# Edge tile, two attention heads side by side, and one layer's memory keys and values as three-pass products

## The chip, the core and the metric

The kernel runs on one core of a Trainium2 chip. Times are device microseconds of that core. The median of the runs of the kernel before the change is 2687.13 us (three runs, 2686.7 to 2687.75).

## What is computed

A network of three layers on one sequence of 512 tokens with 1024 features, in float32: an RWKV-7 layer, a Conformer convolution layer (both with attention to 256 memory tokens and a gated convolutional feed-forward), and a hybrid layer with gated linear attention and a "forget attention" of 8 heads. The parts that the change touches:

```python
memn = rmsnorm(mem, mem_norm_g)                      # mem: 256 x 1024
# memory_cross_attention, in layers 0 and 1:
kv = memn @ w_kv                                     # 1024 x 2048
km = kv[..., :D].reshape(B, -1, XATTN_HEADS, XATTN_HEAD_DIM)
vm = kv[..., D:].reshape(B, -1, XATTN_HEADS, XATTN_HEAD_DIM)
...
# fox_attention, in the hybrid layer: 8 heads of 64 features, blocks of 128 queries
for i in range(S // Q_BLOCK):
    lo, hi = i * Q_BLOCK, (i + 1) * Q_BLOCK
    logits = jnp.einsum('bhqd,bhkd->bhqk', qh[:, :, lo:hi], kh[:, :, :hi]) * scale
    logits = logits + c[:, :, lo:hi, None] - c[:, :, None, :hi]
    mask = jnp.arange(hi)[None, :] <= jnp.arange(lo, hi)[:, None]
    p = jax.nn.softmax(jnp.where(mask, logits, -jnp.inf), axis=-1)
    outs.append(jnp.einsum('bhqk,bhkd->bhqd', p, vh[:, :, :hi]))
```

## The kernel before

Activations lie with features on partitions (8 tiles of 128 x 512, k or m = 0 to 7). A float32 product is made of three matmuls on split operands (`acc3`, L212): each operand is a high part (type float32r) and the rest; high x high (L218), streamed rest x high (L219) and high x rest (L220) add up in one PSUM bank. The names in the trace are in the order output, streamed operand, stationary operand; `ah`, `al`, `bh`, `bl` are the two sides of the pool `act`, `h` the tiles of `home`, `mid` those of the ffn pool, `yh` and `yl` those of `hyo`, `mh` and `ml` the mixed inputs of the first layer.

`Weights` (L34) streams 398 weights tiles of up to 128 x 1024 in a fixed order. SyncE loads each into one of two raw buffers; `_split` (L54) makes the high part on ScalarE (L63) and the rest on VectorE, or on GpSimd for a list of numbers `W_POOL` (L64), into three pairs of buffers; the raw buffer is free after the split. Two kinds of weights, `WHOLE` (L31: memory keys and values of layer 1), aren't split: their raw tile is the operand of one whole float32 matmul (L216), which the profile records as two instructions, and the raw buffer is free when the last of these has read it.

`linear` (L222) runs 8 (or 22) k-steps of `acc3` for each output tile m; a projection of 8 k-steps over 512 columns has 24 matmuls. The framework orders each engine's queue by a simulated timeline within the program's priorities, so TensorE may run matmuls of a later step while an earlier one isn't ready.

Layer 1, `conformer` (L574): `lin` projects the input (conv_w_in), `memory` (L422) loads and scales the memory tokens and sums their squares, here with 32 recorded matmuls of one column (L436); then, for j = 0 to 7, two projections, one step of `memory_keys` (L459: one output tile, 8 products of 256 columns) and a depthwise convolution (L613). Behind them `memory_values` (L481: 32 products of 512 columns, in 8 steps) fills TensorE's time while VectorE and ScalarE do the layer norm over the convolution's result (L662 to L692); conv_w_out follows and needs that result split, chunk by chunk (`al`, L246). Layer 0 has the same keys and values as split products inside `rwkv`, between the steps of its recurrence.

Hybrid layer, `fox_pair` (L945): a generator for two heads (p = 0 to 3). Its steps: projection of q and k (16 k-steps of `acc3`), norms (L962 to L971), then for each head of the pair in turn the scores of all four query blocks (L984) with their softmax (L986 to L993), and the transposes (L1000), copies (L1003) and value products (L1004). A head has 64 of the 128 partitions of q and k, and writes 64 of the 128 partitions of the output. `FOX` (L1631) gives, for each pair, the order of the steps: `c` is the next step of this pair, `Q` and `n` the projection and the norms of the next pair, `G` one projection of the gates (20 in all, 14 of them here).

Addresses, as the framework's allocator gives them to this program: the left-hand pools begin above a reserved scratch for dynamic DMA of 16,384 bytes per partition; weights buffers, `home` (from byte 73,024) and the ffn pool (105,792 to 134,464) begin on multiples of 64. The right-hand pools hang from the top: `act` (147,424 to 229,344; tiles of 2048 bytes) and the first layer's `mix` begin 32 past a multiple of 64. `fb` (L716) takes 32 bytes, so that the pools behind it in the hybrid layer (`hyf`, and `hyo`, 108,128 to 140,896) begin 32 past a multiple of 64 too.

## Time and profile before

| | us |
|---|---|
| median of three runs | 2687.13 |
| the profiled execution, whole | 2691.29 |
| its span, first to last instruction | 2688.5 |
| TensorE busy in it | 2581.6 |
| VectorE, ScalarE, GpSimd busy | 1463.5, 1067.4, 368.3 |

[...] Outside the span lie 2.8 us of the profiled execution. A matmul's duration in the profile overlaps with that of its successor, so the pace of a run of matmuls is read from the starts.

### The profile page before, as it was taken

What the parts mean: (1) busy time and instruction counts of PE and PEld (TensorE: products, weight loads), DVE (VectorE), ACT (ScalarE), POOL (GpSimd) and SP (SyncE); (2) the same over time, 40 slices, a digit from 0 to 9 for tenths busy, and PEclk for the clock granted to TensorE, in tenths of its full rate; (3) what the DMA queues carried; (4) which work ended last, traced back from release to release, by engine and by line L of the source; (5) the groups of instructions that cost most, each with busy time, mean ns of one, the idle gap of its engine ahead of it and who ended that gap; (6) DMA issues with size and microseconds to landing.
All of it is one profiled execution on the core that took longest, in us unless ns stands there. A gap on an engine that the chain in (4) does not pass through costs nothing.

```text
span 2688.5 us, 33718 instructions
## 1 busy us (share of the span) xinstructions
PE 2581.6 (96%) x13436; PEld 2000.3 (74%) x13436; DVE 1463.5 (54%) x2140; ACT 1067.4 (40%) x1709; POOL 368.3 (14%) x362
## 2 busy tenths in 40 slices
PE   6987889899999999999999999999999999999998
PEld 5666767677888888765677888887786677888886
DVE  7584887745677733322654777534324456655522
ACT  6754355534444423312443444323223344433321
POOL 3037422430100001000202000001010000100000
PEclk9997569899999999999999999999998899999999
DMA  3211001321332233443311322232211113322232
GB/s 109 71 51 63 2 17 41 124 94 40 102 99 95 92 92 102 128 124 93 111 63 63 110 94 94 88 91 75 71 63 56 40 40 101 96 94 94 92 93 81
DMA packets 69596, 218.33 MB, mean 81 GB/s; under 512 B 9228, under 2 KB 14749, under 8 KB 69439
## 3 DMA queue, kind: packets, MB, share of 16 engines
q1 hardware_dynamic: 69438, 216.19, 25.6%
q8 instruction: 105, 1.72, 0.3%
q14 instruction: 53, 0.43, 0.1%
HBM read 205.69 MB, written 2.10 MB: 77 GB/s over the span
## 4 chain that ended last, share of the span: by engine, by line
PE 88%; DVE 7%; ACT 2%; POOL 2%; issue 1%; DMA 0%; DVEq 0%; POOLq 0%; ACTq 0%
PE mm L218 24%; PE mm L220 24%; PE mm L219 24%; PE aux L613 2%; PE mm L216 2%; PE aux L321 1%; PE mm L1004 1%; PE mm L1371 1%; POOL inv L1320 1%; POOL inv L1319 1%; PE aux L984 1%; DVE u L1159 1%; DVE h L1289 0%; DVE ml L246 0%; PE aux L1000 0%
## 5 line engine op out<-in xcount | busy, mean ns | idle before, releaser
L63 ACT ACTIVATE wh<-wr 128x1024 fp32r<-128x1024 f32 (+5 forms) x382 | 388.2, 1019 | 788.3 <-PE mm L219 629.0
L64 DVE TENSOR_TENSOR wl<-wr,wh 128x1024 fp32r<-128x1024 f32 (+3 forms) x341 | 401.7, 1179 | 294.8 <-ACT wh L63 292.5
L218 PE MATMUL mm<-ah,wh 128*128 128x512 f32 x1088 | 432.8, 398 | 0.9 <-ACT wh L63 0.9
L219 PE MATMUL mm<-al,wh 128*128 128x512 f32 x1088 | 431.2, 397 | 2.4 <-DVE al L246 2.4
L220 PE MATMUL mm<-ah,wl 128*128 128x512 f32 x1088 | 430.0, 397 | 0.6 <-DVE wl L64 0.5
L218 PE MATMUL mm<-bh,wh 128*128 128x512 f32 (+1 forms) x1000 | 399.7, 401 | 0.0
L219 PE MATMUL mm<-bl,wh 128*128 128x512 f32 (+1 forms) x1000 | 398.1, 398 | 0.0
L220 PE MATMUL mm<-bh,wl 128*128 128x512 f32 (+1 forms) x1000 | 396.6, 398 | 0.0
L218 PEld LDWEIGHTS mm<-ah,wh 128*128 128x128 f32 x1088 | 204.7, 188 | 54.2 <-ACT wh L63 3.7
L219 PEld LDWEIGHTS mm<-al,wh 128*128 128x128 f32 x1088 | 204.8, 188 | 52.8 <-DVE al L246 3.0
L220 PEld LDWEIGHTS mm<-ah,wl 128*128 128x128 f32 x1088 | 204.9, 188 | 50.9 <-DVE wl L64 2.3
L218 PEld LDWEIGHTS mm<-bh,wh 128*128 128x128 f32 (+1 forms) x1000 | 188.6, 189 | 49.9 <-issue 3.9
L269 POOL TENSOR_TENSOR acc<-acc,sq 128x512 f32<-128x512 f32 x55 | 88.3, 1605 | 1001.0 <-ACT sq L268 1000.6
L219 PEld LDWEIGHTS mm<-bl,wh 128*128 128x128 f32 (+1 forms) x1000 | 188.4, 188 | 48.1 <-issue 3.3
L220 PEld LDWEIGHTS mm<-bh,wl 128*128 128x128 f32 (+1 forms) x1000 | 188.1, 188 | 47.9 <-issue 1.7
L381 DVE TENSOR_TENSOR u<-mm,rs 128x512 f32<-128x512 f32 x132 | 90.9, 691 | 176.9 <-PE mm L220 176.7
L64 POOL TENSOR_TENSOR wl<-wr,wh 128x1024 fp32r<-128x1024 f32 (+2 forms) x41 | 98.9, 2413 | 589.6 <-ACT wh L63 589.3
L366 DVE TENSOR_TENSOR x<-x,mm 128x512 f32<-128x512 f32 x56 | 38.5, 687 | 138.8 <-PE mm L220 138.7
L219 PE MATMUL mm<-ml,wh 128*128 128x512 f32 (+1 forms) x224 | 91.4, 409 | 2.4 <-DVE ml L246 2.4
L218 PE MATMUL mm<-mh,wh 128*128 128x512 f32 (+1 forms) x224 | 87.7, 413 | 5.2 <-ACT mh L245 3.7
L220 PE MATMUL mm<-mh,wl 128*128 128x512 f32 (+1 forms) x224 | 90.1, 405 | 1.3 <-DVE wl L64 1.3
L395 ACT ACTIVATE uy<-uy 128x512 f32<-128x512 f32 x66 | 41.6, 632 | 122.5 <-DVE uy L393 122.4
(494 smaller groups left out, 4051.3 us busy)
## 6 DMA issues: line engine op xcount, KB each, us to landing
wr<-ffn_w_in SPq DMA_DIRECT2D x132, 512.0 KB, 3.4
wr<-ffn_w_out SPq DMA_DIRECT2D x48, 448.0 KB, 3.3
wr<-ffn_w_out SPq DMA_DIRECT2D x24, 512.0 KB, 3.5
wr<-hy_g SPq DMA_DIRECT2D x20, 512.0 KB, 3.5
wr<-kv_k SPq DMA_DIRECT2D x16, 512.0 KB, 3.5
wr<-kv_v SPq DMA_DIRECT2D x16, 512.0 KB, 3.5
wr<-xattn_w_q SPq DMA_DIRECT2D x16, 512.0 KB, 3.4
wr<-xattn_w_o SPq DMA_DIRECT2D x16, 512.0 KB, 3.4
```

Source lines behind the costliest of these rows:

```text
L63: self.last_hi = self.nc.scalar.activation(out=hi[:r, :c], in_=t[:r, :c], func=AF.Copy).ins
L64: (self.nc.gpsimd if i in W_POOL else self.nc.vector).tensor_tensor(out=lo[:r, :c], in0=t[:r, :c], in1=f32(hi[:r, :c]), op=ALU.subtract)
L216: self.last_mm = mm(out, lhsT=w[0], rhs=x[0], start=first, stop=last).ins
L218: mm(out, lhsT=w[0], rhs=x[0], start=first, stop=False)
L219: mm(out, lhsT=w[0], rhs=x[1], start=False, stop=False)
L220: mm(out, lhsT=w[1], rhs=x[0], start=False, stop=last)
L269: nc.gpsimd.tensor_tensor(out=self.sq, in0=self.sq, in1=s, op=ALU.add)
L321: self.last_bcast = self.nc.tensor.matmul(ps[:, b * P : (b + 1) * P], lhsT=col[:, b : b + 1].to_broadcast([P, P]), rhs=self.ident, start=T ...
L366: self.nc.vector.tensor_tensor(out=self.x[m], in0=self.x[m], in1=ps, op=ALU.add)
L381: nc.vector.tensor_tensor(out=u, in0=ps, in1=rs, op=ALU.mult)
L395: self.last_silu = nc.scalar.activation(out=y, in_=y, func=AF.Silu if l < 2 else AF.Gelu_apprx_tanh).ins
L613: nc.tensor.matmul(ps[32 * g : 32 * g + 32, 4 * e :], lhsT=w[:, 8 * g + e], rhs=t[:, g, : T - 4 * e], start=(e == 0), stop=(e == 7), skip_ ...
```

## The change

Four things. A spare tile `edge` of 168 float32 per partition is laid at the top of the right-hand side, `fb` takes 16 instead of 8 columns, and the reserved scratch for dynamic DMA is 1,024 instead of 16,384 bytes. `WHOLE` goes: the 16 weights tiles `kv_k1`, `kv_v1` are split like all others, and layer 1's `memory` makes split tiles (twice the bytes) and sums the squares on VectorE, with one pair of column sums on TensorE (`token_sums`). `fox_pair` works on both heads of a pair at once, one query block after the other: scores of block qb for both heads, then transposes, copies and value products of block qb - 1 for both. `FOX` is rewritten for the new steps (norms, four blocks, the last values), with the same 14 gate projections. The order of the weights stays the same. The diff:

```diff
@@ -25,10 +25,6 @@
 
 def f32(ap):
     return ap.bitcast(F32)
-
-
-
-WHOLE = "kv_k1", "kv_v1"
 
 
 class Weights:
@@ -54,10 +50,6 @@
     def _split(self, i):
         key, ap = self.order[i]
         t, r, c = self.raws[i]
-        if key[0] in WHOLE:
-            self.raws[i] = None
-            self.parts.append((t[:r, :c].rearrange("p (a b) -> p a b", b=ap.shape[2]),))
-            return
         hi = self.pool.tile([P, 1024], F32R, tag="whi", bufs=self.bufs, name=f"wh{i}")
         lo = self.pool.tile([P, 1024], F32R, tag="wlo", bufs=self.bufs, name=f"wl{i}")
         self.last_hi = self.nc.scalar.activation(out=hi[:r, :c], in_=t[:r, :c], func=AF.Copy).ins
@@ -98,6 +90,8 @@
         self.ctx, self.tc, self.nc, self.a, self.vec_at = ctx, tc, tc.nc, args, vec_at
         nc = self.nc
         self.keep = ctx.enter_context(tc.tile_pool(name="keep", bufs=1))
+
+        ctx.enter_context(tc.tile_pool(name="edge", bufs=1, side="right")).tile([P, 168], F32, name="edge")
         self.wpool = ctx.enter_context(tc.tile_pool(name="wts", bufs=1))
         self.tmp = ctx.enter_context(tc.tile_pool(name="tmp", bufs=1))
         self.hpool = ctx.enter_context(tc.tile_pool(name="home", bufs=1, reuse_waits="tile"))
@@ -212,9 +206,6 @@
     def acc3(self, out, w, x, first, last):
 
         mm = self.nc.tensor.matmul
-        if len(w) == 1:
-            self.last_mm = mm(out, lhsT=w[0], rhs=x[0], start=first, stop=last).ins
-            return
         mm(out, lhsT=w[0], rhs=x[0], start=first, stop=False)
         mm(out, lhsT=w[0], rhs=x[1], start=False, stop=False)
         mm(out, lhsT=w[1], rhs=x[0], start=False, stop=last)
@@ -419,25 +410,17 @@
 
             self.linear(f"ffn_w_out{l}", KF, list(range(KD)), lambda k: mid[k], out, group=1)
 
-    def memory(self, pool, split):
+    def memory(self, pool):
 
         nc = self.nc
         self.memn = []
         acc = pool.tile([P, MEM], F32, name="macc")
-        ps = None if split else self.aux()
         for k in range(KD):
             raw = self.t512("u", 3, n=MEM)
             nc.sync.dma_start(out=raw, in_=self.a["mem"][:, k, :])
             g = self.vec("g_mem", k)
-            s = self.t512("sq", 2, n=MEM) if k or not split else acc
+            s = self.t512("sq", 2, n=MEM) if k else acc
             nc.scalar.activation(out=s, in_=raw, func=AF.Square)
-            if not split:
-                for b in range(2):
-                    nc.tensor.matmul(ps[:, 2 * k + b : 2 * k + b + 1], lhsT=s[:, b * P : (b + 1) * P], rhs=self.ones[:, 0:1], start=True, stop=True)
-                t = pool.tile([P, MEM], F32, name=f"mn{k}")
-                nc.scalar.activation(out=t, in_=raw, func=AF.Copy, scale=g)
-                self.memn.append((t,))
-                continue
             if k:
                 nc.vector.tensor_tensor(out=acc, in0=acc, in1=s, op=ALU.add)
             hi = pool.tile([P, MEM], F32R, name=f"mnh{k}")
@@ -446,11 +429,7 @@
             nc.vector.scalar_tensor_tensor(out=lo, in0=raw, scalar=g, in1=f32(hi), op0=ALU.mult, op1=ALU.subtract)
             self.memn.append((hi, lo))
         v, self.mcol = self.small(2, "rq"), pool.tile([P, 2], F32, name="mcol")
-        if split:
-            sums = self.token_sums(acc, MEM)
-        else:
-            sums = v
-            nc.vector.tensor_reduce(out=v, in_=ps[:, : 2 * KD].rearrange("p (k t) -> p t k", t=2), axis=AX.X, op=ALU.add)
+        sums = self.token_sums(acc, MEM)
         nc.vector.tensor_scalar(out=v, in0=sums, scalar1=1.0 / D, scalar2=1e-6, op0=ALU.mult, op1=ALU.add)
         self.rsqrt(self.mcol, v, 2)
         self.mrow = acc
@@ -632,7 +611,7 @@
         lin = lambda js: self.linear("conv_w_in", KD, [m for j in js for m in (KD + j, j)], lambda k: xs[k], evict, group=2)
         spreads = {}
         lin([0])
-        self.memory(mp, False)
+        self.memory(mp)
         spreads[0] = spread(0)
         lin([1])
         for j in range(KD):
@@ -713,7 +692,7 @@
             xs, side = self.xs, self.side
             w2 = pool.tile([17, 256], F32, name="aw2")
             nc.sync.dma_start(out=w2, in_=self.a["gla_w2"])
-            fb = pool.tile([P, 8], F32, name="fb")
+            fb = pool.tile([P, 16], F32, name="fb")[:, :8]
             nc.sync.dma_start(out=fb, in_=self.a["fox_b"])
 
             def evict_rs(out, ps, n=T):
@@ -970,18 +949,22 @@
             b = self.pick(self.sel2, i, rows)
             nc.vector.scalar_tensor_tensor(out=qk[i], in0=qk[i], scalar=self.vec("fox_g", i), in1=b, op0=ALU.mult, op1=ALU.mult)
         yield
+
+        heads = [(2 * p + h, slice(h * 64, h * 64 + 64)) for h in range(2)]
+        cbs = []
+        for hd, r in heads:
+            cb = tp.tile([P, T], F32, tag="cb", bufs=2, name=self.nm("cb"))
+            nc.scalar.activation(out=cb, in_=self.bcast_tokens(cq[:, :, hd]), func=AF.Copy)
+            cbs.append(cb)
         po = None
-        for h in range(2):
-            hd = 2 * p + h
-            r = slice(h * 64, h * 64 + 64)
-            b = self.bcast_tokens(cq[:, :, hd])
-            cb = tp.tile([P, T], F32, tag="cb", bufs=2, name=self.nm("cb"))
-            nc.scalar.activation(out=cb, in_=b, func=AF.Copy)
+
+        def scores(qb):
+            n = (qb + 1) * P
+            pss = [self.aux() for _ in heads]
+            for ps, (hd, r) in zip(pss, heads):
+                mmul(ps[:, :n], lhsT=qk[0][r, qb * P : n], rhs=qk[1][r, :n], start=True, stop=True)
             es = []
-            for qb in range(4):
-                n = (qb + 1) * P
-                ps = self.aux()
-                mmul(ps[:, :n], lhsT=qk[0][r, qb * P : n], rhs=qk[1][r, :n], start=True, stop=True)
+            for ps, cb, (hd, r) in zip(pss, cbs, heads):
                 e = tp.tile([P, T], F32, tag="fe", bufs=4, name=self.nm("fe"))
                 nc.vector.scalar_tensor_tensor(out=e[:, :n], in0=ps[:, :n], scalar=cq[:, qb, hd : hd + 1], in1=cb[:, :n], op0=ALU.add, op1=ALU.subtract)
                 d = e[:, qb * P : n]
@@ -992,17 +975,31 @@
                 nc.vector.reciprocal(out=sm, in_=sm)
                 nc.vector.tensor_scalar(out=e[:, :n], in0=e[:, :n], scalar1=sm, scalar2=None, op0=ALU.mult)
                 es.append(e)
-            yield
-            po = po or self.mm()
-            for kb in range(4):
+            return es
+
+        def values(qb, es):
+            n = (qb + 1) * P
+            ts = []
+            for e in es:
                 ps = self.aux()
-                for qb in range(kb, 4):
-                    nc.tensor.transpose(ps[:, (qb - kb) * P : (qb - kb + 1) * P], es[qb][:, kb * P : (kb + 1) * P], self.ident)
-                n = (4 - kb) * P
+                for kb in range(qb + 1):
+                    nc.tensor.transpose(ps[:, kb * P : (kb + 1) * P], e[:, kb * P : (kb + 1) * P], self.ident)
                 t = tp.tile([P, T], F32, tag="fpt", bufs=3, name=self.nm("fpt"))
                 nc.scalar.activation(out=t[:, :n], in_=ps[:, :n], func=AF.Copy)
-                mmul(po[r, kb * P :], lhsT=fv[kb][:, hd * 64 : hd * 64 + 64], rhs=t[:, :n], start=(kb == 0), stop=(kb == 3), skip_group_check=True)
-            if h == 0:
+                ts.append(t)
+            for kb in range(qb + 1):
+                for t, (hd, r) in zip(ts, heads):
+                    mmul(po[r, n - P : n], lhsT=fv[kb][:, hd * 64 : hd * 64 + 64], rhs=t[:, kb * P : (kb + 1) * P], start=(kb == 0), stop=(kb == qb),
+                         skip_group_check=True)
+
+        last = None
+        for qb in range(5):
+            es = scores(qb) if qb < 4 else None
+            if qb:
+                po = po or self.mm()
+                values(qb - 1, last)
+            last = es
+            if qb < 4:
                 yield
         nc.scalar.activation(out=of, in_=po, func=AF.Copy)
         yield
@@ -1514,7 +1511,7 @@
         chunks(0, others)
         pctx.close()
         kctx = ExitStack()
-        self.memory(kctx.enter_context(op("mn0")), True)
+        self.memory(kctx.enter_context(op("mn0")))
         keys = self.memory_keys(0, 1)
 
         def spare(i, ins):
@@ -1628,7 +1625,7 @@
 GATES = [4, 12, 5, 13, 6, 14, 7, 0, 1, 2, 3, 15, 8, 16, 9, 17, 10, 18, 11, 19]
 GLA_G = 2, 0, 1, 0, 1, 1, 0, 1, 0, 0
 
-FOX = "cGQccncGGc", "GQccnGcGc", "GcQccnGGc", "GGcGGccGc"
+FOX = "ccGcQcGcnGc", "cGcQcGcnGc", "cGcQcGcnGc", "cGcGcGcGGc"
 
 
 def hy_keys():
@@ -1755,7 +1752,7 @@
     import concourse.bacc as bacc
     from concourse.bass_utils import run_bass_kernel_spmd
 
-    nc = bacc.Bacc("TRN2", target_bir_lowering=False, num_devices=1)
+    nc = bacc.Bacc("TRN2", target_bir_lowering=False, num_devices=1, dynamic_dma_scratch_size=1024)
     ins, vec_at = arrays({k: np.asarray(v) for k, v in inputs.items()})
     ins = {k: np.ascontiguousarray(v) for k, v in ins.items()}
     args = {k: nc.dram_tensor(k, v.shape, mybir.dt.from_np(v.dtype), kind="ExternalInput").ap() for k, v in ins.items()}
```

## Rows read from the trace of the kernel before

**Rows 1.** The page: busy time of TensorE, and its clock in 40 slices
```profile
PE 2581.6 (96%) x13436; PEld 2000.3 (74%) x13436; DVE 1463.5 (54%) x2140; ACT 1067.4 (40%) x1709; POOL 368.3 (14%) x362
...
PEclk9997569899999999999999999999998899999999
```

**Rows 2.** The page: the chain that ended last, its shares by line
```profile
PE mm L218 24%; PE mm L220 24%; PE mm L219 24%; PE aux L613 2%; PE mm L216 2%; PE aux L321 1%; PE mm L1004 1%; PE mm L1371 1%; POOL inv L1320 1%; POOL inv L1319 1%; PE aux L984 1%; DVE u L1159 1%; DVE h L1289 0%; DVE ml L246 0%; PE aux L1000 0%
```

**Rows 3.** The page: groups of instructions (busy us, mean ns of one, idle before)
```profile
L63 ACT ACTIVATE wh<-wr 128x1024 fp32r<-128x1024 f32 (+5 forms) x382 | 388.2, 1019 | 788.3 <-PE mm L219 629.0
L64 DVE TENSOR_TENSOR wl<-wr,wh 128x1024 fp32r<-128x1024 f32 (+3 forms) x341 | 401.7, 1179 | 294.8 <-ACT wh L63 292.5
L218 PE MATMUL mm<-ah,wh 128*128 128x512 f32 x1088 | 432.8, 398 | 0.9 <-ACT wh L63 0.9
L218 PE MATMUL mm<-bh,wh 128*128 128x512 f32 (+1 forms) x1000 | 399.7, 401 | 0.0
```

**Rows 4.** Timeline (start us, us, engine, line, tiles) of TensorE in layer 0's ffn_w_out
```profile
962.80 0.40 PE L218 MATMUL mm<-bh,wh 128*128 128x512 f32 x1
...
968.40 0.39 PE L218 MATMUL mm<-h,wh 128*128 128x512 f32 x1
...
973.89 0.39 PE L218 MATMUL mm<-mid,wh 128*128 128x512 f32 x1
```

**Rows 5.** Timeline of TensorE in hy_out, six products apart
```profile
2269.53 0.39 PE L218 MATMUL mm<-yh,wh 128*128 128x512 f32 x1
...
2273.73 0.39 PE L218 MATMUL mm<-yh,wh 128*128 128x512 f32 x1
```

**Rows 6.** Chain in order of time (start us, us): one step of layer 1's keys
```profile
1175.57 3.45 PE mm L216 x16
```

**Rows 7.** Timeline of TensorE in layer 0's keys, one product apart
```profile
471.17 0.28 PE L218 MATMUL mm<-mnh,wh 128*128 128x256 f32 x1
...
471.52 0.28 PE L218 MATMUL mm<-mnh,wh 128*128 128x256 f32 x1
```

**Rows 8.** Chain: 4 products of layer 1's values; timeline: layer 0's, 6 products apart
```profile
1270.93 3.44 PE mm L216 x8
...
482.92 0.39 PE L218 MATMUL mm<-wh,mnh 128*128 128x512 f32 x1
...
487.12 0.39 PE L218 MATMUL mm<-wh,mnh 128*128 128x512 f32 x1
```

**Rows 9.** Timeline of TensorE: column sums of layer 1's memory
```profile
1104.38 0.95 PE L436 MATMUL aux<-ones,sq 128*128 128x1 f32 x8
```

**Rows 10.** Chain, then timeline (idle before, releaser), between the values and conv_w_out
```profile
1281.87 3.33 DMA wr<-conv_w_out
...
1295.90 0.80 PE L219 MATMUL mm<-al,wh 128*128 128x512 f32 x1 [2.07 <-DVE al L246]
```

**Rows 11.** Busy time by window: us, PE, PEld, DVE, ACT, POOL, clock, DMA share, GB/s
```profile
1255.47:1297.00 41.53, 37.59 (x107) 18.46 (x107) 27.65 (x43) 27.37 (x39) 2.38 (x1) 0.98 0.39 123
```

**Rows 12.** Waits of TensorE, 1998 to 2258: us in total, times, longest us
```profile
PE aux L1000 <- DVE fe L993: 7.3, 6, 1.9
```

**Rows 13.** Busy time by window, the forget attention (columns as in rows 11)
```profile
1998.00:2258.00 260.00, 251.68 (x1061) 178.14 (x1060) 132.02 (x267) 103.49 (x202) 11.61 (x34) 0.95 0.18 58
```

**Rows 14.** Timeline of TensorE, 422 to 426: products on halves of the array
```profile
422.47 1.17 PE L1371 MATMUL mm<-zr,h 64*128 64x128 f32 x16
423.57 0.66 PE L1377 MATMUL mm<-ident,h 128*128 128x128 f32 x4
424.16 0.69 PE L1415 MATMUL chain<-uv,am 128*64 128x64 f32 x16
424.78 0.68 PE L1423 MATMUL chain<-zr,sh 64*64 64x64 f32 x14
```

**Rows 15.** Line L1004: duration ns min/median/max, first and last start
```profile
L1004 PEld LDWEIGHTS mm<-fpt,fv x64: 132/136/231, 2032.9 to 2230.4; 128*64 128x64 f32 x64
```

**Rows 16.** The page: DMA issues, KB each, median us from issue to landing
```profile
wr<-ffn_w_in SPq DMA_DIRECT2D x132, 512.0 KB, 3.4
```

## Prediction

> **What bounds the kernel now.** I read the page's engine shares and clock first [rows 1], then the chain that ended last [rows 2]: TensorE is busy 96% of the span and three source lines, the three matmuls of `acc3` (L218 to L220), are nearly three quarters of the chain. So a change pays where it shortens what TensorE does, or ends a time in which TensorE waits or runs at the lower clock; the clock line shows two such places, slices 4 to 6 (the first layer's recurrence) and slices 31 and 32, which are the forget attention. Then I looked at each stretch that the diff touches: the spacing of `acc3` matmuls by the tile that they stream [rows 3 to 5], layer 1's memory keys and values and the normalization behind them [rows 6 to 11], the forget attention [rows 12 to 15], and the weight transfers [rows 16].
>
> **Edge tile.** The spare tile takes 672 bytes (168 float32) at the top of each partition. That is 10 times 64 plus 32, so every tile of the right-hand pools, `act` first of all, moves from 32 past a multiple of 64 onto a multiple of 64. The smaller scratch moves the left-hand pools by 15,360 bytes, a multiple of 1024, so nothing changes there except behind `fb`, which grows from 32 to 64 bytes. Does that matter? One loop of the trace streams both kinds of tile against the same weights buffers: `ffn_w_out` of layer 0 reads k = 0 to 7 from `act` and k = 8 to 21 from `home` and the ffn pool, which lie on multiples of 64. The 24 matmuls on `act` start at 962.80 and hand over at 968.40: 5.60 us, 233.3 ns each. The next 24, on `home` tiles, hand over at 973.89: 5.49 us, 228.8 ns [rows 4]. The clock there is full in both. The third kind separates offset from region: `yh`, `yl` of `hyo` lie low, in the range of the ffn pool, but 32 past a multiple of 64, and go at the `act` pace: 6 products (18 matmuls) from 2269.53 to 2273.73, 233.3 ns each [rows 5]. So I take the offset as the cause, 4.5 ns per matmul. Matmuls that stream from `act`: three lines times (1088 + 1000) [rows 3], 6264. 6264 x 4.5 ns = 28 us. All stand in stretches that TensorE bounds, so nothing hides the gain. The first layer's mixed inputs (right side, 576 matmuls) and `hyo` (192) move too: 0 to 3.5 us, I take 2. Together 30; lower bound 0 (offset is not the cause), upper 33.
>
> One row speaks against it: in layer 0's memory values the streamed tile is a weights tile, which lies on a multiple of 64, and still 6 products take 4.20 us, 233.3 ns a matmul [rows 8]. There the stationary tile changes places with the streamed one, so I read it as another case, but it is why the rival below gets a real chance.
>
> [...]
>
> **Memory keys and values of layer 1 as three passes.** Keys: one step of 8 whole products with 256 columns takes 3.45 us, 0.431 a product (each recorded as two instructions) [rows 6]. Layer 0 already does the same products as three passes: from one first pass to the next 0.35 us, 471.17 to 471.52 [rows 7]. 64 products x 0.077 = 4.9 us saved; on TensorE's path, since conv_w_in, keys and the convolution follow each other there without a gap. The added splits (8 times an ACT copy of 1.02 us and a subtraction of 1.18 [rows 3]) lie beside steps in which two projections of 5.6 us and a convolution keep TensorE busy; if that cover were gone, 8 x 2.2 us would show.
>
> Norm of the memory: 32 small matmuls of L436 go; 8 of them take 0.95 us, the tail of the last one under its successor [rows 9], so up to 3.8 us, and 4 instructions of the token sums come (0.5 by the same row). In their place DVE gets 7 additions and 8 subtractions of 256 columns. The trace of before does not show these; by the 1.18 us of a 1024-column subtraction [rows 3] they are 15 x 0.3 = 4.5 us, up to twice that with the fixed part of short operations, beside conv_w_in, which does not wait for them. I take 2.5 saved, bounds 0 and 3.3.
>
> Values: 4 whole products take 3.44 us, 0.86 each, against 0.70 as three passes [rows 8]: 32 x 0.16 = 5.1 us of TensorE. But these values are the filler behind which the normalization of the convolution runs, and that chain does not get shorter. In 1255.47 to 1297 (41.5 us) TensorE is busy 37.6, DVE 27.7 and ACT 27.4 [rows 11], and the stretch already ends in waits: for a weights tile that found no free raw buffer (3.33 us) and for the split of the last normalized chunk (2.07 us) [rows 10]. The change adds about 7 splits there, 1.02 us on ACT and 1.18 on DVE each [rows 3], 8 us on either; ACT and DVE then stand near 36 of 41.5. The raw buffer comes free at the split instead of at the last matmul, so the first wait should go; the second stays or grows. Bounds: 6 gained, 4 lost. I take 2 gained, nearer to the nothing that a chain on ACT and DVE would leave.
>
> **Heads side by side.** Per pair of heads before: all scores of one head, its softmax, transposes, value products, then the other head. At the places where two "c" follow each other in FOX nothing is issued between a head's scores and the transposes that wait for its softmax. [...] After, a gate projection (24 matmuls, 5.6 us by [rows 4]) or more stands between the scores of a query block and its transposes, and it covers a wait of 1.9. It does not at the start of pair 0 ("cc": norm, then scores at once). I let two thirds go, 12 us; bounds 0 and 17.
>
> Both heads' scores use 64 rows of the array each, and both heads' value products 64 columns each. Whether such neighbours run at once is in the trace: 16 instructions of L1371 (8 whole products, 128 columns, the two heads' row halves in turn) take 422.47 to 423.57, 1.10 us; at 0.431 us per 256 columns they would take 1.72 one after the other, so 36% go. For column halves, L1415: 8 products of 64 columns in 0.62 us instead of 0.86, 28% less [rows 14]. Per head the scores stream 128 + 256 + 384 + 512 = 1280 columns, 2.16 us, 17.3 for eight heads; the value products as many. Taking 45% of the scores (longer than L1371's, so the fixed part weighs less) and 36% of the values (128 columns each): 7.8 + 6.2 = 14 us. Bounds: 0, if other matmuls are placed between the two heads, and 17. The softmax operations are the same in number and size. The forget attention gives 12 + 14 = 26; bounds 0 and 34.
>
> [...] Rows first: L1415's 16 instructions with their 16 weight loads take 39 ns each [rows 14], and a weight load of the value products lasts 136 ns [rows 15], so loads run under matmuls of the same rows. [...]
>
> **Sum.** 30 + 4.9 + 2.5 + 2 + 26 = 65 us. The profiled execution has a span of 2688.5 in a run of 2691.29; its span after would be 2623. The median of the runs shown is 2687.13, and I take the difference from it: 2622.
>
> **Rivals.**
> First, the attention gives it back: the scheduler puts projections between the two heads' matmuls, and the block-wise order has eight hand-overs per pair (transposes to ScalarE's copy to products) where each can wait. For it: six waits in the old order, each followed by slow matmuls. Against it: the gates stand in the right places. Then the attention gives 8 instead of 26: 2640. [...] Chance 0.17.
>
> Second, the offset isn't the cause and the edge tile does nothing: 65 - 30 = 35 us, 2652. For it: the weights tile that streams at 233.3 ns [rows 8]. Against: rows 4 and 5. Chance 0.15.
>
> Third, slower: the diff cuts the scratch for dynamic DMA from 16,384 to 1,024 bytes, and 512 KB weights come at one per 5.6 us of TensorE work. A transfer lands in 3.4 us [rows 16] and its buffer is held 2.2 us more by the split [rows 3]; with two raw buffers one weight can come every 2.8 us. The stream decides from the point where landing takes 9 us (then (9 + 2.2) / 2 = 5.6). At 10 us each of some 300 projections would lose 0.5: 150 slower, less the 65: 2772. Nothing in the trace shows that the queue which SyncE issues uses that scratch. Chance 0.04.
>
> Both of the first two together, 2670: 0.04. My forecast: 0.60.
>
> **How the numbers follow.** The forecast's own ends: with every term at its upper bound (33, 4.9, 3.3, 6, 34) 81 us, 2606; with the attention at 14 and the values at -4, 2640. The second rival sits at 2652. 2604 to 2656 leaves out the third rival, the double failure and the tails. A measurement of this kernel can tell about 0.2%, 5 us. All cases but the third rival are faster by more than that, except for a small share of the double failure: faster 0.94, same 0.02, slower 0.04.
>
> **What would show it.** Edge tile: matmuls on `ah`, `bh` tiles at 228.8 ns, so 5.49 us per 24, in every ffn stretch; if they stay at 233.3, the second rival holds. Keys: about 2.8 us per step in place of 3.45, no L216 left. Values: TensorE idle between the last value and conv_w_out no longer than before; if it is longer, DVE and ACT have taken over. Attention: pairs of L984-type matmuls that start within some 10 ns of each other, waits of TensorE for the softmax well under 7.3 us and a granted clock near 1.0 over the stretch. The prediction is wrong most of all if either of the two large terms, 30 and 26, is absent.

## The result and the profile after

| | before | after | after, run again (e11_again) |
|---|---|---|---|
| median, us | 2687.44 | 2657.9 | 2655.63 |
| lowest to highest, us | 2686.7 to 2689.41 | 2650.52 to 2658.11 | 2649.9 to 2656.03 |
| ratio to before, 95% interval | | 0.9882 (0.9864 to 0.99) | 0.9872 (0.9856 to 0.9889) |
| profiled execution, span, us | 2688.5 | 2656.2 | 2648.2 |

The change gives 30 us where 65 were forecast, and the time lies 2 us above the range; the second set of runs lies at its edge. The page of the changed kernel, as [rows 1]:

```profile
PE 2533.9 (95%) x13600; PEld 2008.8 (76%) x13600; DVE 1491.0 (56%) x2169; ACT 1082.7 (41%) x1725; POOL 372.4 (14%) x363
```

TensorE is busy 47.7 us less, but the span is only 32.3 us shorter: 15 us of the work saved came back as idle time. Lining up the first matmul of every weights tile in the two traces says where the 32.3 us lie. The third column takes out what the act tiles alone give there (4.3 ns a matmul, below).

| stretch | change, us | without the act matmuls, us |
|---|---|---|
| start to the first layer's values | -2.8 | -2.8 |
| conv_w_in, layer 1's memory and keys | -4.4 | -3.0 |
| layer 1's values to conv_w_out | +2.8 | +3.4 |
| forget attention | -6.4 | -3.4 |
| all matmuls on act, 6264 x 4.3 ns | | -26.9 |

The third column adds up to 0.4 us more than the span lost. The first row is not an effect of the change: the kernel of e3_heads, which leaves layer 0 as it was, shows -4.0 in the same place, e1_edge none. Each trace is one execution; how far two executions of the changed kernel differ stands under e11_again.

The edge tile. Timeline of TensorE in layer 0's ffn_w_out, with the same hand-overs as [rows 4] (bh to home, home to mid), and in the first projection of the ffn, four weights (96 matmuls) apart:

```profile
953.34 0.39 PE L209 MATMUL mm<-bh,wh 128*128 128x512 f32 x1
...
958.84 0.39 PE L209 MATMUL mm<-h,wh 128*128 128x512 f32 x1
...
964.33 0.39 PE L209 MATMUL mm<-mid,wh 128*128 128x512 f32 x1
...
861.33 0.39 PE L209 MATMUL mm<-ah,wh 128*128 128x512 f32 x1
...
883.30 0.39 PE L209 MATMUL mm<-ah,wh 128*128 128x512 f32 x1
```

The 24 matmuls on bh take 5.50 us, as long as those on home (5.49), where they took 5.60 before; 21.97 us for 96 is 228.9 ns each. So far as forecast. But the mixed inputs and yh, which are on multiples of 64 now too, did not move: by the starts in the trace both go at about 233 ns.

The forget attention. First the waits of TensorE over the stretch (us in total, times, longest), as [rows 12], then the busy time of each engine, as [rows 13]:

```profile
PE aux L986 <- DVE fe L976: 7.0, 5, 2.2
PE aux L1562 <- DVE row L237: 6.5, 4, 2.5
PE aux L1017 <- DVE rp L1013: 3.5, 1, 3.5
```

```profile
1977.00:2231.50 254.50, 236.64 (x1161) 182.44 (x1160) 132.14 (x266) 103.26 (x202) 13.38 (x34) 0.93 0.19 60
```

L986 are the transposes that wait for the softmax: 7.0 us, about as much as before. L1017 and L1562 are two steps of a pair's norms (transposes of the inverse norms, then their spread over the rows): TensorE waits 10 us for them, and did not at all before. The granted clock (1.00 is the full one) fell from 0.95 to 0.93 in this execution.

Layer 1's memory. Waits of TensorE from conv_w_in to conv_w_out, and VectorE's timeline in the first values:

```profile
PE aux L651 <- DVE acc L647: 5.8, 1, 5.8
PE mm L211 <- DVE wl L56: 2.4, 2, 1.9
PE mm L209 <- ACT wh L55: 2.2, 2, 2.0
```

```profile
1245.83 0.69 DVE L647 TENSOR_TENSOR acc<-acc,sq 128x512 f32<-128x512 f32 x1
1246.44 1.22 DVE L56 TENSOR_TENSOR wl<-wr,wh 128x1024 fp32r<-128x1024 f32 x1
1247.57 0.69 DVE L647 TENSOR_TENSOR acc<-acc,sq 128x512 f32<-128x512 f32 x1
1248.17 1.22 DVE L56 TENSOR_TENSOR wl<-wr,wh 128x1024 fp32r<-128x1024 f32 x1
1249.31 2.28 DVE L647 TENSOR_TENSOR acc<-acc,sq 128x512 f32<-128x512 f32 x3
1252.39 1.23 DVE L56 TENSOR_TENSOR wl<-wr,wh 128x1024 fp32r<-128x1024 f32 x1 [0.80 <-ACT wh L55]
1253.53 1.48 DVE L647 TENSOR_TENSOR acc<-acc,sq 128x512 f32<-128x512 f32 x2
```

The layer norm over the convolution's result subtracts the mean (L641), squares on ScalarE and adds the squares on VectorE (L647); TensorE then sums them over the features (L651). L651 stands in TensorE's queue after three steps of the values. Three splits of 1.22 us now stand between the seven additions, and TensorE waits 5.8 us.

### The profile page after: what moved, and what is told of

It is laid out like the page before. It is cut to its first block, busy times and chain, and to the rows that moved or that the text cites. A ratio compares the mean times of both kernels' runs of the same rounds, so it can differ in the third digit from the quotient of the medians.

```text
span 2656.2 us, 34137 instructions
## 1 busy us (share of the span) xinstructions
PE 2533.9 (95%) x13600; PEld 2008.8 (76%) x13600; DVE 1491.0 (56%) x2169; ACT 1082.7 (41%) x1725; POOL 372.4 (14%) x363
## 4 chain that ended last, share of the span: by engine, by line
PE 85%; DVE 8%; ACT 3%; POOL 2%; issue 2%; DMA 1%; SPq 0%; DVEq 0%; POOLq 0%; ACTq 0%
PE mm L209 25%; PE mm L211 24%; PE mm L210 24%; PE aux L592 2%; PE aux L312 1%; POOL inv L1316 1%; POOL inv L1317 1%; ACT wh L55 1%; PE mm L1368 1%; DVE wl L56 1%; PE mm L992 1%; DVE u L1156 0%; DVE h L1286 0%; PE aux L986 0%; DVE ml L237 0%
## 5 line engine op out<-in xcount | busy, mean ns | idle before, releaser
L55 ACT ACTIVATE wh<-wr 128x1024 fp32r<-128x1024 f32 (+2 forms) x398 | 404.6, 1020 | 782.6 <-PE mm L210 623.6
L56 DVE TENSOR_TENSOR wl<-wr,wh 128x1024 fp32r<-128x1024 f32 (+3 forms) x356 | 421.8, 1187 | 289.8 <-ACT wh L55 284.2
L209 PE MATMUL mm<-ah,wh 128*128 128x512 f32 x1088 | 426.1, 394 | 2.3 <-ACT wh L55 2.2
```

Source lines behind the costliest of these rows:

```text
L55: self.last_hi = self.nc.scalar.activation(out=hi[:r, :c], in_=t[:r, :c], func=AF.Copy).ins
L56: (self.nc.gpsimd if i in W_POOL else self.nc.vector).tensor_tensor(out=lo[:r, :c], in0=t[:r, :c], in1=f32(hi[:r, :c]), op=ALU.subtract)
L209: mm(out, lhsT=w[0], rhs=x[0], start=first, stop=False)
```

## Experiments

The kernels e1 to e3 each make one part of the change to the kernel before; the time of before beside them was 2688.75 us.

**e1_edge: the spare tile alone.**

```diff
+        ctx.enter_context(tc.tile_pool(name="edge", bufs=1, side="right")).tile([P, 168], F32, name="edge")
         self.wpool = ctx.enter_context(tc.tile_pool(name="wts", bufs=1))
```

> The kernel before with the 168-column spare tile alone. The trace after the change shows the matmuls on ah, bh tiles starting 228.9 ns apart instead of 233.3, and those on the mixed inputs and on yh unchanged. Theory A, the tile's gain is all there and the other parts gave next to nothing together: 6264 x 4.4 ns = 28 us less than before, about 2659. Rival, the pace of 228.9 ns came with the smaller scratch or the other weights order in time: 0 to 5 us less.

2660.53 us, ratio 0.9901 (0.9879 to 0.9924), 28.2 us less. Theory A holds. Scratch and `fb` were left alone here, so they have no part in it.

**e2_memory: keys and values as three passes, with the smaller scratch.** The edit is the part of the diff on `WHOLE`, `_split`, `acc3` and `memory`.

> The kernel before with layer 1's memory keys and values as three passes and the smaller scratch (without which the tiles don't fit), nothing else. In the changed kernel's trace the keys take 4.0 us and the column sums 2.8 us less of TensorE, but a wait of 2.5 us for weights splits appears near the first keys and one of 5.8 us for the layer norm's sums inside the values. Theory A, the waits belong to this part: -3 to +3 us, about no change. Rival, the waits come from the other parts: 9 us less, as predicted. If the smaller scratch slowed transfers, it would show here as well, as more than 5 us slower.

2684.45 us, ratio 0.9987 (0.9978 to 0.9997), 4.3 us less by the medians and 2 in the trace of its profiled execution (5.3 won up to the first value, 3.3 lost behind it). The waits are all there: 5.7 us for the norm's sums, 1.5 for the weights near the first keys. The part brings its own waits (theory A). The scratch costs nothing that can be seen.

**e3_heads: both heads at once, with the new FOX.** The edit is the part of the diff on `fox_pair` and `FOX`.

> The kernel before with fox_pair of both heads at once and its new FOX order, nothing else. The changed kernel's trace shows 18 us less of TensorE work in scores, value products and transposes, and 9.5 us more of waits, most of them inside the norms of the next pair, and more time at the lower clock. Theory A, the waits belong to this order: 2 to 6 us less than before in all. Rival, they come from a shift that the other parts cause: 15 to 26 us less.

2683.12 us, ratio 0.9977 (0.9966 to 0.9988), 5.6 us less. Its waits are those of the changed kernel to 0.1 us for the norms (6.5 and 3.4 us). Theory A holds. The three ratios multiply to 0.9865, inside the intervals of the changed kernel: the parts add up. What is missing from the forecast is missing in e3 (5.6 of 26 us) and in e2 (4.3 of 9.4), while e1 has 28.2 of 30.

**e4_map: where the streamed tile may lie.** A kernel of matmuls alone: `xh`, `xl` stream from r bytes past a multiple of 1024, the stationary `wh`, `wl` begin s bytes past one.

```python
for s, rs in PLAN:
    for r in [512] + rs:
        x = [t[n][:, r // 4 : r // 4 + T] for n in ("xh", "xl")]
        for k in range(KD):
            w = [t[n][:, s // 4 + k * P : s // 4 + (k + 1) * P] for n in ("wh", "wl")]
            nc.tensor.matmul(ps, lhsT=w[0], rhs=x[0], start=k == 0, stop=False)
            nc.tensor.matmul(ps, lhsT=w[0], rhs=x[1], start=False, stop=False)
            nc.tensor.matmul(ps, lhsT=w[1], rhs=x[0], start=False, stop=k == KD - 1)
```

> None of the network is computed: only runs of 24 matmuls (8 products of three passes, 512 columns) whose streamed tile lies 0 to 992 bytes past a multiple of 1024 in steps of 32, against stationary tiles 0, 320, 64 and 32 past one. My prediction's reading (a multiple of 64 is enough): 228.8 ns apart at 0, 64, 128, ... and 233.3 at 32, 96, .... The reading of the changed kernel's trace, where 0, 448 and 640 go at 233 and only 320 at 229: fast at 320 and perhaps at 64, 576, 832 (64 past a multiple of 256), slow at 0, 128, 448, 640. Third, the offset relative to the stationary tile counts: the fast places move when that moves by 320.

Timeline of TensorE: the first matmuls of some groups of 24; a group lasts to the next row, but for the gaps behind m160s0x and m288s0x (m128s64x streams from 128 against a stationary tile at 64):

```profile
36.27 0.40 PE L43 MATMUL m128s0x<-xh,wh 128*128 128x512 f32 x1
...
41.87 0.40 PE L43 MATMUL m160s0x<-xh,wh 128*128 128x512 f32 x1
...
58.69 0.39 PE L43 MATMUL m256s0x<-xh,wh 128*128 128x512 f32 x1
...
64.15 0.40 PE L43 MATMUL m288s0x<-xh,wh 128*128 128x512 f32 x1
...
292.35 0.39 PE L43 MATMUL m0s64x<-xh,wh 128*128 128x512 f32 x1
...
297.95 0.39 PE L43 MATMUL m128s64x<-xh,wh 128*128 128x512 f32 x1
...
303.45 0.40 PE L43 MATMUL m256s64x<-xh,wh 128*128 128x512 f32 x1
```

Streamed from 128, a group takes 5.60 us against a stationary tile at 0 and 5.50 against one at 64; streamed from 0, it takes 5.60 against 64, while 256 against 0 takes 5.46. The third theory holds. Mean ns from start to start, by streamed minus stationary address modulo 256, over all 68 places that were tried:

```text
difference mod 256    stationary 0    stationary 320   stationary 64   stationary 32
0                     226.6 - 227.7   227.5 - 228.5    227.3 - 227.7   227.7
64                    229.3           229.6            229.0 - 229.3   229.3
all others            233.1 - 234.1   232.7 - 233.5    233.0 - 233.6   232.3 - 233.4
```

The traces of the network say the same. Their weights tiles lie on multiples of 256, so that a tile streamed against them has its own place modulo 256 as the difference. Before: act is at 224 (233.3), home and the ffn pool at 64 (229.1), yh at 96 (233.4). After: act at 64 (229.0), the mixed inputs at 192 (about 233), yh at 128 (232.9), and the streamed weights of the memory values at 192 against their stationary tile (233.3).

How the two operands lie to each other is worth some 6 ns in 233 in e4_map. The runs show the addresses and the pace, not the mechanism.

**e5_edge8 and e6_edge56: two other sizes, on the kernel before.** `[P, 8]` and `[P, 56]` in place of `[P, 168]`; the time of before beside them was 2688.94 us.

> The kernel before with a spare tile of 8 columns (32 bytes): the act tiles then lie on a multiple of 64, at 960 past a multiple of 1024, 192 past one of 256. Reading of the prediction (a multiple of 64 is enough): as with 168 columns, 228.9 ns on ah, bh and 28 us less, about 2660. Reading of the map (streamed less stationary address has to be 0 or 64 modulo 256): 233.3 ns on ah, bh, and no change but 2 us on the mixed inputs, which come to 64 past a multiple of 256: 0 to 3 us less.

> The kernel before with a spare tile of 56 columns (224 bytes): act comes to a multiple of 256, the mixed inputs to 128 past one. Reading of the map: ah, bh at 228.9 ns, and the 192 matmuls of the forget and gated attention's values that stream a weights tile against a stationary bh tile go at 228.9 too (with 168 columns they stayed at 233.3): 28 to 29 us less. If only the offset of the streamed tile counted, these 192 would stay at 233.3; if the place 320 past 1024 were needed, nothing would change.

```profile
862.63 0.40 PE L219 MATMUL mm<-ah,wh 128*128 128x512 f32 x1
...
885.03 0.40 PE L219 MATMUL mm<-ah,wh 128*128 128x512 f32 x1
```

```profile
859.80 0.39 PE L219 MATMUL mm<-ah,wh 128*128 128x512 f32 x1
...
881.56 0.39 PE L219 MATMUL mm<-ah,wh 128*128 128x512 f32 x1
```

The first fence is e5_edge8, the second e6_edge56, both four weights apart in the ffn: 22.40 us (233.3 ns) and 21.76 us (226.7 ns). e5 gives 2686.31 us, ratio 0.9991 (0.9981 to 1.0): a multiple of 64 is worth nothing by itself here, and what is won is about the 2 us of the mixed inputs, which do reach 229 ns. e6 gives 2646.0 us, 0.9845 (0.9831 to 0.986): 42.9 us less, 14 more than I expected. I had carried over 228.9 ns; at a difference of 0 act goes at 227.2 in this trace, so 6264 x 1.7 ns = 11 of these 14 us are explained; the other 3 are not, but are about what separates two sets of runs of one kernel. The 192 matmuls that stream weights, and whose streamed tile did not move, go at 227.9 instead of 233.3: it is the difference that counts.

**e8_order: another order of the steps, on e3_heads.**

```diff
-FOX = "ccGcQcGcnGc", "cGcQcGcnGc", "cGcQcGcnGc", "cGcGcGcGGc"
+FOX = "cGcQcncGcGc", "cQcncGcGGc", "cQcncGcGGc", "cGcGcGcGGc"
```

> The kernel of e3_heads with another FOX order: norms of the next pair two blocks before the end (cQcncG...), so that a projection stands behind their transposes in TensorE's queue. Theory: the waits of 2.4 to 3.5 us for the normalized rows and the lower clock behind them come from this order, not from working on two heads: the waits for rows go, idle time of TensorE in the stretch falls from 18 us to 8 or less, and the kernel is 6 to 14 us faster than e3_heads, 12 to 18 below before. Rival, two heads at once need the waits (ScalarE and VectorE cannot deliver faster): other waits take their place and the time stays within 3 us of e3_heads.

```profile
PE aux L1007 <- DVE fe L997: 5.3, 4, 2.4
PE mm L1013 <- ACT fpt L1009: 2.9, 3, 2.1
```

```profile
1994.00:2239.00 245.00, 235.50 (x1153) 179.84 (x1152) 132.36 (x267) 102.36 (x202) 10.63 (x34) 0.94 0.18 60
```

2672.98 us, ratio 0.9945 (0.993 to 0.996): by the medians 16 us less than before and 10 less than e3_heads, by the ratios 15 and 9, and in the two traces the stretch is 7 shorter. The waits for the norms (L1038, L1583 in this kernel) are gone; idle time falls from 17.5 to 9.5 us. So those waits came from the order. (First fence: waits of TensorE in the stretch; second: busy time, columns as in [rows 11].) The waits for the softmax stay, those for the copies of the transposed tiles grow from 0.7 to 2.9 us, and the granted clock is 0.94 in both: that part the order does not cure.

**e7_pool, e9_pool2, e12_nosplit: the wait in the values, all on e2_memory.** e7 and e9 send splits to GpSimd, e12 leaves their low part out.

```diff
-W_POOL = (... 123, 166, 174, ...)
+W_POOL = (... 123, 165, 166, 167, 168, 174, ...)    # e7_pool
+W_POOL = (... 123, 166, 168, 169, 170, 174, ...)    # e9_pool2
-        lo = self.pool.tile([P, 1024], F32R, tag="wlo", bufs=self.bufs, name=f"wl{i}")
+        lo = hi if i in (168, 169, 170) else self.pool.tile([P, 1024], F32R, tag="wlo", bufs=self.bufs, name=f"wl{i}")   # e12_nosplit
```

> The kernel of e2_memory with three more weights numbers split by GpSimd (the first, third and fourth of layer 1's memory values; the second is there already). Theory: TensorE waits 5.7 us for the layer norm's sums because three splits of 1.22 us stand between VectorE's additions and the cover is 3 x 2.86 us in place of 10.5; with the splits gone from VectorE the wait falls by about 3.7 us, to 2, and with it 1 or 2 us at the lower clock: 3 to 5 us less than e2_memory. Rival, VectorE waits for something else (ScalarE's squares): the wait stays near 5.7. Third, GpSimd's splits of 2.4 us slow VectorE as one did before (an operation of 0.7 us took 2.45): less than 2 us is won.

> The kernel of e2_memory with the splits of weights 168, 169 and 170 on GpSimd: these are the three that stand between VectorE's additions in the trace of e2_memory (in e7_pool only one of them was moved, and the broadcast of the norm went to another place of TensorE's queue; here the queue's order stays that of e2_memory). Theory: the wait of 5.7 us for the layer norm's sums falls by the 3.6 us of the three splits, to about 2; 2 to 4 us less than e2_memory. Rival, GpSimd's splits of 2.4 us hold VectorE's additions up by as much: the wait stays at 4 or more.

> The kernel of e2_memory without the low part of weights 168, 169 and 170: the subtraction of these three splits is left out on every engine and the third pass of their products reads the high part again, so part of the memory values is computed wrong; TensorE's work and queue are unchanged. Theory: in e2_memory the layer norm's sums come late because these three subtractions of 1.22 us stand between VectorE's additions, in e9_pool2 because GpSimd's slowed the additions. Then the wait of 5.7 us falls to about 2.0, which is the 10.5 us of cover before less the 8.6 of three steps after. Rival, the squares on ScalarE (behind the high parts of the same weights) hold the additions up: the wait stays above 4.

e7 gives 2691.52 us, 1.0011 (1.0002 to 1.0021). It settles nothing: two splits stayed between the additions, and half of the broadcast of the norm moved behind the last value in TensorE's queue, so that conv_w_out waits 6.2 us more. e9 keeps the queue: 2687.4 us, 0.9994 (0.9985 to 1.0003), no gain over e2_memory. VectorE's timeline of e9 with the first of GpSimd's splits, then that of e12 with the wait of TensorE:

```profile
1253.49 2.41 POOL L59 TENSOR_TENSOR wl<-wr,wh 128x1024 fp32r<-128x1024 f32 x1 [20.00 <-ACT wh L58]
1254.29 2.16 DVE L648 TENSOR_TENSOR acc<-acc,sq 128x512 f32<-128x512 f32 x1
...
1256.55 2.69 DVE L648 TENSOR_TENSOR acc<-acc,sq 128x512 f32<-128x512 f32 x1
...
1259.34 3.08 DVE L648 TENSOR_TENSOR acc<-acc,sq 128x512 f32<-128x512 f32 x4
...
1262.99 2.42 DVE L648 TENSOR_TENSOR acc<-acc,sq 128x512 f32<-128x512 f32 x1 [0.57 <-ACT sq L646]
```

```profile
1258.43 1.48 DVE L649 TENSOR_TENSOR acc<-acc,sq 128x512 f32<-128x512 f32 x2
1260.91 2.29 DVE L649 TENSOR_TENSOR acc<-acc,sq 128x512 f32<-128x512 f32 x3 [0.99 <-ACT sq L647]
1263.77 1.49 DVE L649 TENSOR_TENSOR acc<-acc,sq 128x512 f32<-128x512 f32 x2 [0.57 <-ACT sq L647]
```

```profile
PE aux L653 <- DVE acc L649: 3.4, 1, 3.4
```

GpSimd's three splits of e9 run from 1253.5 to 1255.9, 1256.3 to 1258.7 and 1262.5 to 1264.9. The three additions that meet one take 2.16, 2.69 and 2.42 us and end some 0.55 us behind it; the four between them take 0.69 each. The wait grows to 7.7 us. The rival held there. In e12 the wait is 3.4 us, between the 2.0 of my theory and the 4 of the rival, and both have a share. Of e2_memory's 5.7 us, 1.9 are the shorter cover (10.5 us of values before, 8.6 now), 2.3 the three subtractions, and 1.6, by the two idle times in the fence, ScalarE's squares, which stand behind the high parts of the same weights. The time of e12, 2683.03 us (0.9978, 0.9965 to 0.9991), is not clearly below e2_memory's: the rest of the layer norm still stands between this place and conv_w_out.

**e10_best: what the runs point to.** On the changed kernel: a spare tile of 56 columns, a gap of 192 bytes ahead of `home`, one of 128 ahead of the mixed inputs, `fb` of 64 columns, so that every streamed tile of the three-pass products has a difference of 0; the FOX of e8_order; the splits of e9_pool2.

> The changed kernel with every streamed tile of three-pass products brought to the same place modulo 256 as the stationary one (spare tile of 56 columns, 192 bytes ahead of home, 128 bytes ahead of the mixed inputs, fb of 64 columns), the FOX order of e8_order and the splits of e9_pool2. Against the changed kernel: act 6264 x 1.7 ns = 11 us, mixed inputs 576 x 5.9 = 3.4, yh 192 x 5.9 = 1.1, home and mid 1008 x 1.7 = 1.7, memory values 384 x 6 = 2.3, order 10, splits 2 to 4: 31 to 33 us, about 2626. If the parts share a limit (transfers, the clock), under half of it: above 2642.

2629.8 us (2619.75 to 2635.99), ratio to before 0.9772 (0.9744 to 0.98), the fastest kernel here; the changed kernel beside it:

> The changed kernel as it is, once more beside the others. The three parts alone gave 28.2, 4.3 and 5.6 us, 38 together, and the changed kernel 29.5. If the parts add up and the difference is the spread between executions: 2648 to 2655 here. If they hinder each other: 2658 again.

2655.63 us, beside a before of 2690.8: between the two expectations. Its trace differs from that of the changed kernel above in the forget attention (columns as in [rows 11], from the same first to the same last matmul, the changed kernel first):

```profile
1977.78:2230.71 252.93, 235.07 (x1154) 181.16 (x1152) 131.35 (x266) 103.26 (x202) 13.38 (x34) 0.93 0.19 59
1975.78:2222.82 247.04, 229.30 (x1153) 177.18 (x1152) 131.24 (x266) 103.23 (x202) 13.38 (x34) 0.95 0.18 60
```

The idle time is the same (17.9 and 17.7 us), and so is each wait; busy time is 5.8 us less, at a higher granted clock. So 6 us of what the trace above lacks in this stretch go with the lower clock of that execution: the change in the stretch is -6 us in one execution and -12 in the other.

By the starts in its trace, e10's products on act, home, mid, yh, the mixed inputs and the values go at 226.7 to 228.1 ns. Against the changed kernel beside it that is 26 of the 31 to 33 us expected. TensorE still waits 7.8 us in the values, as in e9_pool2, so the splits gave nothing, 2 to 4 us less than expected; the rest of the shortfall lies within the 16 us that the four runs spread over.

## Why the prediction was wrong

In the first trace of the changed kernel 35 of the 65 us did not come (its first layer, which the change does not touch, left out): 23 in the attention (17 in the execution of e11_again), 5 in the values, 4 in the keys and sums, 3 in the edge tile.

**Edge tile: the size came out, the cause did not.** 28.2 us for 28 on act. The step that failed is "So I take the offset as the cause". What counts is not the streamed tile's own multiple of 64 but its distance to the stationary tile modulo 256: in e4_map 226.6 to 229.6 ns at a distance of 0 or 64, 232.3 to 234.1 at all others. [rows 4, 5] fit both readings, since home is at 64 and act and yh at neither 0 nor 64. The row that told them apart was [rows 8], the weights tile on a multiple of 64 that streams at 233.3 ns; I wrote it off as "another case" because the operands change places, and the change of places was the point. 168 columns happen to put act at 64, the second-best place: that the size came out is luck. The 2 us on the mixed inputs and hyo, from the same step, were not there. The second rival, that the tile does nothing, is refuted: e1 is clear of zero.

**Keys and sums: right on TensorE.** The keys' matmuls fell from 28.0 to 24.0 us of TensorE (4.9 forecast), the column sums from 3.15 to 0.36 (2.5). The step that failed is "on TensorE's path, since conv_w_in, keys and the convolution follow each other there without a gap": with less work on that path a gap opened. The words "beside conv_w_in, which does not wait for them" held for the splits of the memory tokens as far as the traces show: the 15 operations of 256 columns on VectorE took 0.42 to 0.48 us each, some 6.8 us, within the 4.5 to 9 that I had. TensorE waited for a weights load, as ScalarE's and SyncE's timelines of the changed kernel show (start, us, idle time and releaser):

```profile
1098.13 1.06 ACT L55 ACTIVATE wh<-wr 128x1024 fp32r<-128x1024 f32 x1 [4.99 <-DMA wr<-conv_w_in]
...
1088.15 4.31 SPq L580 DMA_DIRECT2D cu<-bl  x7
1092.50 1.67 SPq L47 DMA_DIRECT2D wr<-conv_w_in  x1
```

The load was issued at 1092.5, behind the transfers that spread the convolution's input, and landed at 1098.1; TensorE, with 2.8 us of column sums less ahead of it, got there first and waited 2.5 us. The granted clock from 1092 to 1132 is 0.96, where the 39 us around the same place had 1.00 before. That the missing work opened the gap is read from the timelines; no run tests it. Of the queues that a step is moved against, I had looked at none but TensorE's.

**Values: inside the bounds, on the wrong side.** 3.4 us lost where I took 2 won (6 to -4). The reason was the right one, a chain on VectorE and ScalarE behind the values that grows, but I looked for it at the end of the stretch. It came out in the middle, where the sums stand in TensorE's queue at a fixed place, three steps behind the first value. Behind the wait the granted clock is down as well: it is 0.50 from 1256 to 1262, where the matmuls of the values start 0.43 us apart instead of 0.23, and 0.80 over 15 us (columns as in [rows 11]), so that the 32 products fell by 2.8 us (28.3 to 25.5) where I had 5.1:

```profile
1256.00:1271.00 15.00, 15.00 (x60) 12.37 (x61) 6.52 (x13) 6.84 (x9) 0.00 (x0) 0.80 0.24 79
```

**Attention: scores and value products fell by more than forecast, and waits and the clock took most of it back.** From start to start, with the waits taken out:

| us of TensorE in the stretch | before | after | forecast |
|---|---|---|---|
| scores | 21.7 | 14.2 | -7.8 |
| value products | 24.7 | 14.2 | -6.2 |
| transposes of the softmax, squares of the norms | 22.1 | 18.1 | none |
| broadcasts, picks and transposes of the norms | 13.2 | 18.6 | none |
| projections (of which the act tiles give -3.0) | 169.3 | 170.1 | none |
| waits | 8.3 | 17.9 | two thirds gone |

Where nothing stands between the matmuls of two heads, they start 6 to 7 ns apart and run at once: two score products of 512 columns take 1.06 us together at a granted clock of 1.00, where one took 1.05 before, and two of 384 columns 0.84. I had put scores and value products at 17.3 us each, where the kernel before spends 21.7 and 24.7. The scores lost 35% of that instead of 45%, the value products 43% instead of 36%. The value products with 160 recorded matmuls and 160 loads take 10.5 us less than with 64 and 64. The rows that grow are the broadcasts and picks, which stand behind the new waits; in e8_order, without these waits, they take 11.5 us.

The step that failed is "After, a gate projection (24 matmuls, 5.6 us by [rows 4]) or more stands between the scores of a query block and its transposes", with "I let two thirds go": the waits for the softmax stayed at 7.0 of 7.3 us, and 10 us of waits for the norms, for which I had no term, came on top. The 12 us are two thirds of 17: 7.3 of waits and 10 for the lower clock behind them. No run shows the 10 by itself; what the traces show is a granted clock before of 0.50 from 2030 to 2042, behind the waits of pair 0, and of 0.95 over the stretch, and after of 0.65 from 1997 to 2010, 0.77 to 0.79 behind the later waits, and 0.93 over the stretch. At the start of pair 0, the place that I had named as uncovered, TensorE now waits 7 us where it waited 2.8, most of it for the norms (idle time in brackets):

```profile
1994.17 1.01 PE L1017 MATMUL aux<-ident,rp 128*32 128x128 f32 x4 [3.45 <-DVE rp L1013]
1996.58 1.22 PE L1562 MATMUL aux<-row,sel 64*128 64x512 f32 x2 [1.39 <-DVE row L237]
...
2005.05 0.33 PE L986 MATMUL aux<-ident,fe 128*128 128x128 f32 x1 [1.94 <-DVE fe L976]
```

In the other pairs the projection does stand there in the program. In TensorE's queue, where a pair ends and the next one begins, it does not:

```profile
2044.02 0.39 PE L211 MATMUL mm<-bh,wl 128*128 128x512 f32 x1
2044.24 0.60 PE L1017 MATMUL aux<-ident,rp 128*32 128x128 f32 x4
2047.30 1.22 PE L1562 MATMUL aux<-row,sel 64*128 64x512 f32 x2 [2.46 <-DVE row L237]
2048.45 1.97 PE L986 MATMUL aux<-ident,fe 128*128 128x128 f32 x8
...
2055.59 0.92 PE L965 MATMUL aux<-qk,qk 64*128 64x128 f32 x6
2057.92 0.33 PE L986 MATMUL aux<-ident,fe 128*128 128x128 f32 x1 [1.41 <-DVE fe L976]
...
2058.98 0.50 PE L209 MATMUL mm<-bh,wh 128*128 128x512 f32 x1
```

The only projection behind "n" has been used up by 2044.24, between the squares of the norms and their transposes; the spread over the rows (L1562) then waits bare, and the projection that is to cover the next pair's softmax comes after the transposes that wait for it. In the order before, two projections or more followed the norms, and 3.3 to 8.0 us of them lay between L1020 and L1565 of a pair; I had counted the old order's waits and not what its projections covered. e8_order puts it back, at pair 0 too, and gets 7 to 10 of the missing us. This was the rival "the attention gives it back", by another mechanism than the hand-overs that I named for it.

## What to carry to other kernels

Before costing a reordering, list for every chain on another engine the TensorE work that stands behind it in the queue as issued, in the old order and in the new one; a cover that nobody had to name before is the first thing that a rewrite loses. A row that contradicts the cause is not to be set aside as another case: it is the cheapest test there is. Work taken from TensorE in a place where it fills a wait came back as wait in the values here, and the subtractions that pay for it lengthened the chain that it covers (1.9 and 2.3 of the 5.7 us that TensorE waits in e2_memory). And one trace is one execution: with the same waits, the forget attention took 253 us in one and 247 in another.

## What was not expected of the hardware

In these runs a float32r matmul of 512 columns whose streamed tile lies a multiple of 256 bytes from the stationary one went at 227 to 228 ns, 64 bytes past that at 229 to 230, and anywhere else that was tried at 232 to 234 (e4_map, e5_edge8, e6_edge56). On this kernel the best place is worth 43 us of 2689, by one spare tile. An addition of two tiles on VectorE went from 0.69 us to between 2.2 and 2.7 where a subtraction of 2.4 us on GpSimd ran beside it, and ended some 0.55 us behind that (e9_pool2).
